# A fourth accumulator bank for the down projection, and both ends of the output projection reordered

## The chip, the cores and the metric

The kernel runs on one NeuronCore of a Trainium2 chip. The metric is the device time of one execution in microseconds (us). Matmuls run on TensorE (PE in the rows), elementwise work on VectorE (DVE), ScalarE (ACT) and GpSimd (POOL); SyncE (SP) and ACT issue the loads and stores. Matmul results land in PSUM, which this kernel uses as eight accumulators (banks) of 512 fp32 columns.

## What is computed

One decoder block over 2048 positions of width 1024, in fp32:

```
h = modulate(rms_norm(x, norm1_g[l]), shift1, scale1)
...
att_out = rms_norm(att, att_onorm_g[l])
mix = jnp.concatenate([hg_out, att_out], axis=-1) @ w_out[l]
x = x + gate1[:, None, :] * mix
h = modulate(rms_norm(x, norm2_g[l]), shift2, scale2)
a, u = jnp.split(h @ w_gate_up[l], 2, axis=-1)
x = x + gate2[:, None, :] * ((jax.nn.silu(a) * u) @ w_down[l])
return rms_norm(x, final_g)
```

`hg_out` is the output of a gated linear recurrence (512 columns), `att` that of a dilated attention (512 columns); `w_gate_up` has 2 x 2816 columns.

## The kernel before

Activations lie transposed: features on the partitions, positions along the free axis. Each fp32 matmul is made of three (lines 881 to 883 for most of the kernel, 1123 to 1125 for down): both operands are split into a high part (a cast on ACT) and a low part (a subtraction, `tt`, line 79, on DVE or POOL), and high x high, high x low and low x high are added in a bank. For a weight the parts are `whi` and `wlo`, made by `parts` from a loaded `wraw`.

The recurrence and the attention fill the first 1384 us. They leave their outputs in DRAM, `hg_d` and `at_d`, in four chunks of 512 positions. Then come:

**The output projection**, 1385 to about 1591 us: for each chunk c and each of eight row tiles j one bank (`psG`, four banks) takes 12 matmuls with the recurrence's half (`hgs`) and 12 with the attention's half (`ats`). The attention's half is first normed by `att_half`: a sum over partitions on TensorE (`norm_sum`, tile `nps`, in a bank of its own), `rstd` by Ln and Exp on ACT, the scaling on DVE (line 321), and the two parts of each of four tiles (cast `mx<-mraw` on ACT, line 291, and a subtraction on DVE). For chunk 0 four products are begun with the recurrence's half alone. Each finished bank is added to x on DVE (line 995), squared on ACT (line 305) and summed into `ssq`; at the start of the next chunk `norm_out` turns the chunk's rows into the FFN's input, which goes to DRAM as `h2_d`. In the last chunk the first operands of the FFN are loaded (`hr`, by `load_block`) and split by 28 *pieces* (`operand_pieces`), which run mostly on DVE; some of them first add or subtract operands, `hv<-hr` or `hr<-hr`.

**The FFN**, to the end: three pairs p of two position blocks (four blocks of 344 columns, then two of 336), and for each pair 11 steps g. A step has two `gate_up`, each of seven products of 12 matmuls (a 2 x 2 block scheme with sums and differences of weights, `wt`, and of operands), and one `down` for the step before: 16 groups of six matmuls, each in a bank (`psD`, three banks), which a residual step on DVE adds to x:

```
ps = pp_d.tile([P, CH], F32, name="psD", tag="psD", bufs=3)[:, 0:n]
...
dve.scalar_tensor_tensor(x, ps, ga2[:, j:j + 1], x, ALU.mult, ALU.add)
```

A `gate_up` ends with two `finish`: gate times up on DVE (`hm<-hm`), and the product's two parts (`ahi` on ACT, `alo<-hm,ahi` on DVE), which the next down needs. For the second `gate_up` of a step the parts are handed on as `late`, and `down` issues them at its fourth group (`soon`).

Each engine works through one queue in order. A scheduler sets that order when the program is built, from the order in which the source issues the steps, from priorities and from hints (`issue_after`, `keep_in_program_order`); the buffer counts of the pools (`bufs`) set when a tile is free again.

Of the kernel before, what the change touches and what calls it, by code (L numbers as in the profile page):

```python
# [19 lines left out]
P = 128  # L20
S = 2048
D = 1024
# [27 lines left out]
def hybrid_block(ctx, tc, xT, small, cst, w_ada, w_ft, w_tk, w_out, w_gu, w_dn, out):  # L50
# [233 lines left out]
    def load_mix(src):  # L284
        raw = cpool["mr"].tile([P, CH], F32, name="mraw", tag="mraw", bufs=6)
        nc.sync.dma_start(out=raw, in_=src)
        return raw

    def two_parts(dst, src, eng=dve, copy=act.copy):
        hi, lo = dst  # L290
        copy(hi, src)
        tt(eng, lo, src, hi.bitcast(F32), ALU.subtract)

    def norm_sum(ssq, n):
# [13 lines left out]
    def mix_tile(name):  # L308
        return cpool["mr"].tile([P, CH], F32, name="a" + name, tag="a" + name, bufs=2 if name == "sq" else 1)
# [7 lines left out]
    def att_half(dst, raws, ssq):  # L317
        rstd = mix_tile("sq")
        rstd_of(norm_sum(ssq, CH), rstd, 512)
        for k, raw in enumerate(raws):  # L320
            dve.scalar_tensor_tensor(raw, raw, sm[:, V_AG + k:V_AG + k + 1], rstd, ALU.mult, ALU.mult)
            two_parts(dst[k], raw)
# [358 lines left out]
    with ax:  # L681
# [30 lines left out]
        def branch_steps(hd):  # L712
# [36 lines left out]
            def drain():  # L749
                for br, bk, src in evac:  # L750
# [11 lines left out]
                    if hd == 7 and br == 0:  # L762
                        finish_head(hd, bk)
                        if bk == 0:
                            at(1, lambda: early.update(raws=[load_mix(at_d[k][0]) for k in range(4)]))
                            at(ATT, lambda: early.update(ssq=att_squares(early["raws"])))
# [66 lines left out]
        for hd in range(8):  # L833
# [13 lines left out]
            if hd == 7:  # L847
                hgs, raws, ws = {}, [], []
# [3 lines left out]
                def begin():  # L852
# [5 lines left out]
                    raws.extend(load_mix(hg_d[k][0]) for k in range(4))  # L858
                    raws.extend(raw_w(w_out[j][:, z * 512:(z + 1) * 512]) for j, z in FIRST)
                after[LAG + 2] = [begin]  # L860
                for k in range(4):
# [68 lines left out]


    h = {}
    with ExitStack() as wl:
        for nm in ("hg1", "at0", "xw0", "xw1", "at1", "wsc"):
            c_pool(nm, wl)
        for nm in ("pp_d", "ppc", "pp_n"):
            c_pool(nm, space=PSUM)

        def w_tile(name, bufs=2):
            return cpool["wsc"].tile([P, CH], F32, name=name, tag=name, bufs=bufs)  # L940

        def load_xw(c):
            x = cpool[f"xw{c % 2}"].tile([P, KT, CH], F32, name="xw", tag="xw")
# [4 lines left out]
        def norm_out(c, x, ssq):  # L948
            rstd = w_tile("rstd", 1)
            rstd_of(norm_sum(ssq, CH), rstd, D)  # L950
            for k in range(KT):
# [3 lines left out]
                nc.scalar.dma_start(out=h2_d[c][:, k, :], in_=v)  # L955

# [16 lines left out]
        for j in range(4):  # L973
            begun.append(psG(CH))
            product(begun[-1], wq[0, j][0], hgs[0], True, False)
        ats[0] = half_of("at0")
        att_half(ats[0], early["raws"], early["ssq"])
        pieces = []
        for i, (c, j) in enumerate(order):
# [11 lines left out]
            if c and j == 0:  # L991
                with tc.issue_after(end):
                    norm_out(c - 1, xs[c - 1], boxes[c - 1]["ssq"])
            x = xs[c][:, j, :]
            dve.scalar_tensor_tensor(x, ps, ga1[:, j:j + 1], x, ALU.mult, ALU.add)
            add_square(box, x, lambda name: w_tile(name, 1 if name == "ssq" else 2))
# [11 lines left out]
            if c + 1 < NCH:  # L1008
                if j == 3:
                    xs[c + 1] = load_xw(c + 1)  # L1010
                if j == 4:
                    ats[c + 1] = half_of(f"at{(c + 1) % 2}")
                    with tc.issue_after(end):
                        att_half(ats[c + 1], raws, ssq)
            if c == NCH - 1:
                if j == 0:
                    wr.close()
                    c_pool("hp", side="right")
                if j == 1:
                    n = BLK[0][1]  # L1020
                    tiles = [cpool[nm].tile([P, KT, CH], F32R if nm == "at0" else F32, name="hr", tag=tag)
                             for nm, tag in (("at0", "mx"), ("xw0", "xw"))]
                    tiles[0] = tiles[0].bitcast(F32)
# [245 lines left out]
```

## Time and profile before

| | |
|---|---|
| Median of 3 runs | 3075.54 us (3074.14 to 3080.18) |
| Profiled execution, its own time | 3070.15 us |
| Its span, first to last instruction | 3068.4 us |
| PE busy | 2850.8 us, 93% of the span, 16308 instructions |
| DVE busy | 2067.0 us, 67% |
| POOL busy | 1408.4 us, 46% |
| ACT busy | 1312.5 us, 43% |
| Mean granted TensorE clock | 0.979 of full speed |

Busy shares are means over the whole span. The chain that ended last is almost all PE's: its lines 881 to 883 come first, then 1123 to 1125. What a change in one stage is worth has to be read from that stage's waits.

### The profile page before, as it was taken

The page shows a single profiled execution, that of the slowest core. Times are in us where ns is not written, and L with a number is a line of the kernel's source. Part 1 is how long each engine was busy: PE and PEld are TensorE (multiplying, and loading weights), DVE is VectorE, ACT ScalarE, POOL GpSimd, SP SyncE. Part 2 cuts the span into 40 slices and gives each one's busy share as a digit, 9 for nine tenths or more (in the row PEclk, how much of TensorE's full clock was granted, in tenths as well). Part 3 has the DMA queues.
Part 4 walks back from the last instruction along what each step waited for, and adds up shares of the span by engine and source line. Part 5 has one row for each costly group of instructions (what it writes and reads, how often), then busy time and mean ns, then how long its engine had stood idle before and what let it go on. Part 6 is the DMA issues. An engine that isn't in the chain of part 4 may idle for free. (4 is left out here: it accounts for less than half of the span.)

```text
span 3068.4 us, 45120 instructions
## 1 busy us (share of the span) xinstructions
PE 2850.8 (93%) x16308; PEld 2595.3 (85%) x16308; DVE 2067.0 (67%) x3781; ACT 1312.5 (43%) x2388; POOL 1408.4 (46%) x1074
## 2 busy tenths in 40 slices
PE   6999998889899999998989999999999998999998
PEld 4777776667678999987769999998999998999997
DVE  7567566667644665666776666678667669776676
ACT  4533423334432565665554333345333335443334
POOL 5344422244533232320036566566566655665664
PEclk9999999999999999999989999999999999999999
DMA  6301336400238674537744222123232212231221
GB/s 243 118 35 42 117 124 219 151 32 32 83 115 218 143 165 101 134 106 237 260 161 157 73 80 79 60 83 106 96 116 73 80 66 95 83 113 63 81 71 67
DMA packets 212031, 343.32 MB, mean 112 GB/s; under 512 B 24784, under 2 KB 97360, under 8 KB 208720
## 3 DMA queue, kind: packets, MB, share of 16 engines
q1 hardware_dynamic: 201984, 322.35, 33.3%
q10 hardware_dynamic: 9824, 18.09, 1.6%
q8 instruction: 128, 2.10, 0.3%
q14 instruction: 95, 0.78, 0.1%
HBM read 281.39 MB, written 58.98 MB: 111 GB/s over the span
## 5 line engine op out<-in xcount | busy, mean ns | idle before, releaser
L79 POOL TENSOR_TENSOR wlo<-wraw,whi 128x512 fp32r<-128x512 f32 (+1 forms) x540 | 846.7, 1590 | 535.8 <-ACT whi L86 305.9
L881 PE MATMUL psG<-chi,whi 128*128 128x344 f32 (+1 forms) x1848 | 596.8, 323 | 15.6 <-DVE hm L79 7.4
L883 PE MATMUL psG<-chi,wlo 128*128 128x344 f32 (+1 forms) x1848 | 593.0, 321 | 3.5 <-POOL wlo L79 3.5
L882 PE MATMUL psG<-clo,whi 128*128 128x344 f32 (+1 forms) x1848 | 594.6, 322 | 0.0
L277 ACT CAST whi<-wraw 128x512 fp32r<-128x512 f32 x520 | 311.2, 619 | 423.7 <-issue 191.8
L1123 PE MATMUL psD<-ahi,whi 128*128 128x344 f32 (+1 forms) x1056 | 345.7, 327 | 43.8 <-DVE xc L1126 43.7
L1126 DVE SCALAR_TENSOR_TENSOR xc<-psD,mods,xc 128x344 f32<-128x344 f32 (+1 forms) x528 | 295.2, 569 | 110.0 <-PE psD L1125 109.8
L881 PEld LDWEIGHTS psG<-chi,whi 128*128 128x128 f32 x1848 | 351.2, 190 | 20.7 <-DVE hm L79 6.8
L883 PEld LDWEIGHTS psG<-chi,wlo 128*128 128x128 f32 x1848 | 350.5, 190 | 4.3 <-POOL wlo L79 4.1
L882 PEld LDWEIGHTS psG<-clo,whi 128*128 128x128 f32 x1848 | 350.2, 190 | 0.0
L79 POOL TENSOR_TENSOR wlo<-wt,whi 128x512 fp32r<-128x512 f32 x132 | 194.3, 1481 | 334.7 <-ACT whi L277 263.3
L1125 PE MATMUL psD<-ahi,wlo 128*128 128x344 f32 (+1 forms) x1056 | 337.3, 319 | 0.0
L1124 PE MATMUL psD<-alo,whi 128*128 128x344 f32 (+1 forms) x1056 | 336.3, 318 | 0.0
L79 DVE TENSOR_TENSOR hm<-hm,psG 128x344 f32<-128x344 f32 (+1 forms) x330 | 165.8, 503 | 244.3 <-PE psG L883 243.6
L511 PE MATMUL psA<-hhi,whi 128*128 128x512 f32 x640 | 262.7, 411 | 1.7 <-ACT hhi L396 1.7
L512 PE MATMUL psA<-hlo,whi 128*128 128x512 f32 x640 | 259.5, 406 | 0.2 <-DVE hlo L79 0.2
L513 PE MATMUL psA<-hhi,wlo 128*128 128x512 f32 x640 | 259.1, 405 | 0.0
L1123 PEld LDWEIGHTS psD<-ahi,whi 128*128 128x128 f32 x1056 | 198.8, 188 | 59.9 <-DVE xc L1126 55.5
L79 POOL TENSOR_TENSOR hd<-hb 128x256 f32<-128x256 f32 x192 | 134.2, 724 | 165.5 <-DVE hy L624 82.3
L1124 PEld LDWEIGHTS psD<-alo,whi 128*128 128x128 f32 x1056 | 199.0, 188 | 0.5
L1125 PEld LDWEIGHTS psD<-ahi,wlo 128*128 128x128 f32 x1056 | 198.9, 188 | 0.0
L277 ACT CAST whi<-wt 128x512 fp32r<-128x512 f32 x132 | 81.2, 617 | 258.9 <-DVE wt L79 139.0
(237 smaller groups left out, 6023.5 us busy)
## 6 DMA issues: line engine op xcount, KB each, us to landing
wraw<-in_w_gu SPq DMA_DIRECT2D x264, 256.0 KB
wraw<-in_w_dn SPq DMA_DIRECT2D x132, 256.0 KB
adaw<-in_w_ada SPq DMA_DIRECT2D x48, 512.0 KB
wraw<-in_w_ft SPq DMA_DIRECT2D x40, 512.0 KB
wraw<-in_w_tk SPq DMA_DIRECT2D x32, 512.0 KB
qk_d<-st SPq DMA_DIRECT2D x64, 256.0 KB
v<-v_d SPq DMA_DIRECT2D x16, 1024.0 KB
wraw<-in_w_out SPq DMA_DIRECT2D x64, 256.0 KB
```

What stands on the lines that cost most here:

```text
L79: return eng.tensor_tensor(o, a, b, op)
L277: copy(hi, raw)
L511: pe.matmul(ps, whi[:, ws], hhi[:, k, :], start=k == 0, stop=False)
L512: pe.matmul(ps, whi[:, ws], hlo[:, k, :], start=False, stop=False)
L513: pe.matmul(ps, wlo[:, ws], hhi[:, k, :], start=False, stop=k == 7)
L881: pe.matmul(ps, w[0][:, ws], hi, start=start and k == 0, stop=False, skip_group_check=True)
L882: pe.matmul(ps, w[0][:, ws], lo, start=False, stop=False, skip_group_check=True)
L883: last = pe.matmul(ps, w[1][:, ws], hi, start=False, stop=stop and k == 3, skip_group_check=True)
L1123: pe.matmul(ps, w[z][0][:, ws], ahi, start=z == 0, stop=False)
L1124: pe.matmul(ps, w[z][0][:, ws], alo, start=False, stop=False)
L1125: pe.matmul(ps, w[z][1][:, ws], ahi, start=False, stop=z == 1)
L1126: dve.scalar_tensor_tensor(x, ps, ga2[:, j:j + 1], x, ALU.mult, ALU.add)
```

## The change

1. `finish` no longer multiplies at once: the two products of gate and up become the first two entries of `late`, the parts the last two, and `down` takes one entry of `soon` at each group from the third on. (In the first `gate_up` of a step all four run at its end, as before.)
2. `psD` has four banks. The bank of `nps` is given up, and `norm_sum` takes one of the four in turn.
3. Start of the output projection: the first three attention tiles of chunk 0 are loaded and squared earlier; their norm is issued behind the second begun product, not the fourth, and the recurrence's tiles of the next chunk are split only after the attention's parts (`last_part`).
4. End: the `hr` tiles get room of their own and are loaded at j = 0 of the last chunk, four pieces follow each later j, the first product of the FFN (`gate_first`) is issued with the end of the stage, and the eight steps of `norm_out` for the last chunk come behind the first `gate_up`, with a load of ACT's function table.
5. Tiles share names (`rstd` lies in `ssq`, the FFN's small tiles in the projection's pool), and x tiles of odd chunks lie in a pool that the FFN goes on using.

```diff
-        raw = cpool["mr"].tile([P, CH], F32, name="mraw", tag="mraw", bufs=6)
+        raw = cpool["mr"].tile([P, CH], F32, name="mraw", tag="mraw", bufs=7)
...
     def norm_sum(ssq, n):
-        ps = cpool["pp_n"].tile([P, CH], F32, name="nps", tag="nps", bufs=1)[:, 0:n]
+        ps = cpool["pp_d"].tile([P, CH], F32, name="nps", tag="psD", bufs=4)[:, 0:n]
         pe.matmul(ps, ones, ssq, start=True, stop=True)
         return ps
+
+    def rstd_from(ps, dst, width, load):
+
+
+        if load:
+            with tc.issue_after(silu[0]):
+                tc.keep_in_program_order(act.preload_act_table_set("natural_log_exp_and_others"))
+        i = act.activation(dst, ps, AF.Ln, bias=eps, scale=1.0 / width)
+        if load:
+            tc.keep_in_program_order(i)
+        act.activation(dst, dst, AF.Exp, scale=-0.5)
...
                     raws.extend(load_mix(hg_d[k][0]) for k in range(4))
+                    early["raws"].extend(load_mix(at_d[k][0]) for k in range(3))
                     raws.extend(raw_w(w_out[j][:, z * 512:(z + 1) * 512]) for j, z in FIRST)
...
+    def gate_first(f, h, n):
+
+        raws = [raw_w(w_gu[i][:, z * 512:(z + 1) * 512]) for i, z in ((f, 0), (FT + f, 0), (FT + f, 1), (f, 1))]
+        ps = psG(n)
+        return raws, ps, product(ps, parts(raws[0]), h["11"])
...
-            product(begun[-1], wq[0, j][0], hgs[0], True, False)
-        ats[0] = half_of("at0")
-        att_half(ats[0], early["raws"], early["ssq"])
+            end = product(begun[-1], wq[0, j][0], hgs[0], True, False)
+            if j == 1:
+                ats[0] = half_of("at0")
+                with tc.issue_after(end):
+                    rstd = att_rstd(box["ssq"])
+        last_part = att_half(ats[0], early["raws"], rstd)
...
                 if j < 2:
-                    for k in (2 * j, 2 * j + 1):
-                        two_parts(hgs[c + 1][k], raws[k])
+
+                    with tc.issue_after(last_part):
+                        for k in (2 * j, 2 * j + 1):
+                            two_parts(hgs[c + 1][k], raws[k])
...
                 else:
-                    for _ in range(min(5, len(pieces))):
+                    for _ in range(4):
                         pieces.pop(0)()
-        norm_out(NCH - 1, xs[NCH - 1], box["ssq"])
-        while pieces:
-            pieces.pop(0)()
+        assert not pieces
+        first = gate_first(0, h, n)
...
-            def finish(si, u):
-
-                tt(dve, si, si, u, ALU.mult)
-                res.append(a_tile(n))
-                late.append(lambda: two_parts(dst, si))
-                dst = res[-1]
...
+            def finish(i, si, u):
+
+                def mul():
+                    tt(dve, si, si, u, ALU.mult)
+                    res.append(a_tile(n))
+                late.insert(i, mul)
+                late.append(lambda: two_parts(res[i], si))
+
...
-                if step == 4:
-                    for f in soon:
-                        f()
+                if step > 1 and soon:
+                    soon.pop(0)()
...
-                ps = pp_d.tile([P, CH], F32, name="psD", tag="psD", bufs=3)[:, 0:n]
+                ps = pp_d.tile([P, CH], F32, name="psD", tag="psD", bufs=4)[:, 0:n]
...
-                acts = [gate_up(2 * g, h, n)[0]]
+                acts = [gate_up(2 * g, h, n, first=None if p or g else first)[0]]
+                if not p and not g:
+                    steps = norm_out(NCH - 1, xs_last, boxes[NCH - 1]["ssq"], True)
```

The built order on three engines shows what the scheduler makes of it. On DVE, at one down call in the steady loop of the first pair (`hm<-hm` is gate times up, `hm<-hm,psG` takes a product's bank in, `xc<-psD,mods,xc` is the residual step), the rows before are:

```order
L79 TENSOR_TENSOR hm<-hm,psG 128x344
L79 TENSOR_TENSOR hm<-hm 128x344
L1126 SCALAR_TENSOR_TENSOR xc<-psD,mods,xc 128x344
L79 TENSOR_TENSOR alo<-hm,ahi 128x344
L1126 SCALAR_TENSOR_TENSOR xc<-psD,mods,xc 128x344
L79 TENSOR_TENSOR alo<-hm,ahi 128x344
L1126 SCALAR_TENSOR_TENSOR xc<-psD,mods,xc 128x344 x14
```

The rows of the changed kernel at the same place, on DVE:

```order
L79 TENSOR_TENSOR hm<-hm 128x344
L79 TENSOR_TENSOR hm<-hm,psG 128x344
L79 TENSOR_TENSOR hm<-hm 128x344
L1169 SCALAR_TENSOR_TENSOR xc<-psD,mods,xc 128x344
L79 TENSOR_TENSOR alo<-hm,ahi 128x344
L1169 SCALAR_TENSOR_TENSOR xc<-psD,mods,xc 128x344
L79 TENSOR_TENSOR alo<-hm,ahi 128x344
L1169 SCALAR_TENSOR_TENSOR xc<-psD,mods,xc 128x344 x14
```

Nothing moved here: the products stand ahead of the first residual step in both, and the parts between the first three.

On ACT, at the start of the output projection (`at_d` and `rl` belong to the attention's last head, `asq` is the attention's norm, `whi` a weight's part, `mx` a part of either half), before:

```order
L824 ACTIVATE rl<-rl 64x512
L827 DMA at_d_3_120<-ao 64x512
L277 CAST whi<-wraw 128x512
L291 CAST mx<-mraw 128x512 x2
L277 CAST whi<-wraw 128x512 x3
L91 ACTIVATE asq<-nps,eps 128x512
L92 ACTIVATE asq<-asq 128x512
L291 CAST mx<-mraw 128x512 x6
```

And of the changed kernel, on ACT at the same place:

```order
L840 ACTIVATE rl<-rl 64x512
L843 DMA at_d_3_120<-ao 64x512
L277 CAST whi<-wraw 128x512 x2
L91 ACTIVATE asq<-nps,eps 128x512
L92 ACTIVATE asq<-asq 128x512
L291 CAST mx<-mraw 128x512
L277 CAST whi<-wraw 128x512
L291 CAST mx<-mraw 128x512 x2
L277 CAST whi<-wraw 128x512
L291 CAST mx<-mraw 128x512 x5
```

The norm (lines 91 and 92) moved ahead of all casts, and the two casts of chunk 1's recurrence tiles that stood ahead of it went behind the attention's.

On SP, which issues the loads, at the end of the output projection (`w_out` and `w_gu` are the weights of the projection and of gate and up, `hr` the first operands of the FFN), before:

```order
L271 DMA wraw<-in_w_out 128x512 x9
L945 DMA xw<-in_xT 128x512 x8
L271 DMA wraw<-in_w_out 128x512 x7
L894 DMA hr<-h_d_125 128x8x344
L271 DMA wraw<-in_w_out 128x512 x4
L271 DMA wraw<-in_w_gu 128x512 x2
L894 DMA hr<-h_d_125 128x8x168
L894 DMA hr<-h_d_126 128x8x176
L271 DMA wraw<-in_w_gu 128x512 x9
```

And of the changed kernel, on SP at the same place:

```order
L271 DMA wraw<-in_w_out 128x512 x9
L984 DMA xc<-in_xT 128x512 x8
L271 DMA wraw<-in_w_out 128x512 x11
L271 DMA wraw<-in_w_gu 128x512 x5
L917 DMA hr<-h_d_125 128x8x344
L917 DMA hr<-h_d_125 128x8x168
L917 DMA hr<-h_d_126 128x8x176
L271 DMA wraw<-in_w_gu 128x512 x2
```

All three operand loads now stand together, behind five weight loads of gate_up; before, the first stood among the projection's weights and the other two behind two.

## Rows read from the trace of the kernel before

**Rows 1.** Windows: length, busy us (x instructions) by engine, PE clock, DMA share, GB/s.

```profile
1423.60:1576.60 153.00, 153.00 (x651) 122.06 (x649) 110.23 (x173) 91.78 (x155) 3.98 (x4) 1.00 0.70 239
1576.60:1621.00 44.40, 28.66 (x126) 25.36 (x126) 35.13 (x53) 24.58 (x44) 23.36 (x16) 0.77 0.28 95
1621.00:3068.40 1447.40, 1376.67 (x8613) 1354.88 (x8611) 1026.30 (x1513) 556.74 (x1079) 876.96 (x618) 0.99 0.26 86
```

**Rows 2.** Waits of PE from 1600 us on: total us, times, longest.

```profile
PE psD L1123 <- DVE xc L1126: 43.7, 39, 2.4
```

**Rows 3.** Timeline of PE, a down call: start, us, instruction [idle before <-releaser].

```profile
1918.75 0.32 PE L1123 MATMUL psD<-ahi,whi 128*128 128x344 f32 x1
...
1921.42 0.31 PE L1125 MATMUL psD<-ahi,wlo 128*128 128x344 f32 x1
1923.05 0.43 PE L1123 MATMUL psD<-ahi,whi 128*128 128x344 f32 x1 [1.32 <-DVE xc L1126]
...
1924.11 0.43 PE L1123 MATMUL psD<-ahi,whi 128*128 128x344 f32 x1
```

**Rows 4.** Timeline of DVE, the same call.

```profile
1919.93 1.60 DVE L79 TENSOR_TENSOR hm<-hm 128x344 f32<-128x344 f32 x1
...
1922.42 0.57 DVE L1126 SCALAR_TENSOR_TENSOR xc<-psD,mods,xc 128x344 f32<-128x344 f32 x1
...
1923.49 0.57 DVE L1126 SCALAR_TENSOR_TENSOR xc<-psD,mods,xc 128x344 f32<-128x344 f32 x1
```

**Rows 5.** Timeline of DVE, then of PE, a call of the second pair.

```profile
2191.69 0.51 DVE L79 TENSOR_TENSOR hm<-hm 128x344 f32<-128x344 f32 x1
...
2193.72 0.42 PE L1123 MATMUL psD<-ahi,whi 128*128 128x344 f32 x1 [0.20 <-DVE xc L1126]
2195.24 0.42 PE L1123 MATMUL psD<-ahi,whi 128*128 128x344 f32 x1 [0.32 <-DVE xc L1126]
```

**Rows 6.** Timeline of POOL, the call of rows 3.

```profile
1919.67 1.49 POOL L79 TENSOR_TENSOR wlo<-wt,whi 128x512 fp32r<-128x512 f32 x1 [0.38 <-ACT whi L277]
```

**Rows 7.** Timeline of PE, the start of the output projection.

```profile
1396.10 1.02 PE L296 MATMUL nps<-assq,ones 128*128 128x512 f32 x2
1404.77 2.07 PE L881 MATMUL psG<-mx,whi 128*128 128x512 f32 x4 [7.65 <-ACT mx L291]
...
1423.61 1.02 PE L296 MATMUL nps<-assq,ones 128*128 128x512 f32 x2
```

**Rows 8.** Timeline of ACT, then of DVE, the same stretch.

```profile
1397.15 0.69 ACT L91 ACTIVATE asq<-nps,eps 128x512 f32<-128x512 f32 x1 [0.47 <-PE nps L296]
...
1403.58 2.69 ACT L291 CAST mx<-mraw 128x512 fp32r<-128x512 f32 x5 [5.08 <-DMA mraw<-hg_d]
...
1398.53 2.08 DVE L321 SCALAR_TENSOR_TENSOR mraw<-mraw,sm,asq 128x512 f32<-128x512 f32 x3 [1.12 <-ACT asq L92]
```

**Rows 9.** Timeline of PE, the end of the output projection.

```profile
1583.31 0.80 PE L883 MATMUL psG<-mx,wlo 128*128 128x512 f32 x1 [6.50 <-DVE wlo L79]
...
1594.64 0.65 PE L881 MATMUL psG<-chi,whi 128*128 128x344 f32 x1 [2.15 <-ACT whi L277]
```

**Rows 10.** Timeline of PE, a down call of the last pair.

```profile
2768.34 0.42 PE L1123 MATMUL psD<-ahi,whi 128*128 128x336 f32 x1 [1.68 <-DVE xc L1126]
```

**Rows 11.** Timeline of DVE, the operand pieces' start and the weight sum behind them.

```profile
1569.56 0.94 DVE L79 TENSOR_TENSOR hv<-hr 128x344 f32<-128x344 f32 x2 [3.97 <-DMA hr<-h_d]
...
1591.66 0.68 DVE L79 TENSOR_TENSOR wt<-wraw 128x512 f32<-128x512 f32 x1
```

**Rows 12.** Timeline of SP's loads, the same stretch.

```profile
1561.00 6.17 SPq L271 DMA_DIRECT2D wraw<-in_w_gu  x4
```

**Rows 13.** Timeline of ACT, a table load.

```profile
1608.88 1.28 ACT L1088 ACT_TABLE_LOAD   x1 [0.39 <-ACT hv L954]
```

**Rows 14.** Timeline of DVE, then of PE, the end of the kernel.

```profile
3053.48 4.06 DVE L79 TENSOR_TENSOR ssq<-ssq,sq 128x336 f32<-128x336 f32 x4
...
3057.60 1.49 PE L296 MATMUL nps<-ssq,ones 128*128 128x336 f32 x2 [5.73 <-DVE ssq L79]
```

More of the change, by code (lines that the diff above doesn't have):

```diff
@@ L315, in att_squares, with att_rstd, att_half @@
         return box["ssq"]
-    def att_half(dst, raws, ssq):
+    def att_rstd(ssq):
         rstd = mix_tile("sq")
         rstd_of(norm_sum(ssq, CH), rstd, 512)
+        return rstd
+    def att_half(dst, raws, rstd):
         for k, raw in enumerate(raws):
             dve.scalar_tensor_tensor(raw, raw, sm[:, V_AG + k:V_AG + k + 1], rstd, ALU.mult, ALU.mult)
-            two_parts(dst[k], raw)
+            last = two_parts(dst[k], raw)
+        return last
     with ExitStack() as ab:
@@ L764, in drain @@
                         if bk == 0:
-                            at(1, lambda: early.update(raws=[load_mix(at_d[k][0]) for k in range(4)]))
-                            at(ATT, lambda: early.update(ssq=att_squares(early["raws"])))
+                            at(1, lambda: early["raws"].append(load_mix(at_d[3][0])))
+                            at(ATT, lambda: square(3))
                 evac.clear()
@@ L858, in begin @@
                     raws.extend(load_mix(hg_d[k][0]) for k in range(4))
+                    early["raws"].extend(load_mix(at_d[k][0]) for k in range(3))
                     raws.extend(raw_w(w_out[j][:, z * 512:(z + 1) * 512]) for j, z in FIRST)
                 after[LAG + 2] = [begin]
+                for k in range(3):
+                    after.setdefault(PRE - 1 + k, []).append(lambda k=k: square(k))
                 for k in range(4):
@@ L946, in load_xw, with norm_out, apply @@
             return x
[L948 to L951, printed above, removed]
+        def norm_out(c, x, ssq, load=False):
+            rstd = w_tile("ssq")
+            rstd_from(norm_sum(ssq, CH), rstd, D, load)
+            def apply(k):
                 v = w_tile("hv")
@@ L955, in norm_out @@
                 nc.scalar.dma_start(out=h2_d[c][:, k, :], in_=v)
+            return [lambda k=k: apply(k) for k in range(KT)]
         wq = {(0, j): [None, None] for j in range(4)}
@@ L1017, in hybrid_block @@
                     wr.close()
+                    w0.close()
+                    c_pool("hr", wl)
                     c_pool("hp", side="right")
-                if j == 1:
                     n = BLK[0][1]
-                    tiles = [cpool[nm].tile([P, KT, CH], F32R if nm == "at0" else F32, name="hr", tag=tag)
-                             for nm, tag in (("at0", "mx"), ("xw0", "xw"))]
-                    tiles[0] = tiles[0].bitcast(F32)
+                    tiles = [cpool["hr"].tile([P, KT, T], F32, name="hr", tag=f"hr{b}") for b in range(2)]
                     pieces = operand_pieces(h, [load_block(t, h2_d, b) for b, t in enumerate(tiles)], n,
@@ L1043, in a_tile, with gate_up @@
             return tuple(wk_a.tile([P, T], F32R, name=nm, tag=nm, bufs=8)[:, 0:n] for nm in ("ahi", "alo"))
-        def x_tiles(p):
-            return [cpool[f"xpc{p % 2}"].tile([P, KT, T], F32, name="xc", tag=f"xc{i}") for i in range(2)]
         def load_blocks(p, src_d):
-            return [load_block(t, src_d, 2 * p + i) for i, t in enumerate(x_tiles(p))]
+            pair = x_pair(p, 2 * T).rearrange("p (i k t) -> p i k t", i=2, t=T)
+            return [load_block(pair[:, i], src_d, 2 * p + i) for i in range(2)]
         pace = []
-        def gate_up(f, h, n, wait=False):
-            b11, b12 = raw_w(w_gu[f][:, 0:512]), raw_w(w_gu[FT + f][:, 0:512])
-            b22, b21 = raw_w(w_gu[FT + f][:, 512:1024]), raw_w(w_gu[f][:, 512:1024])
+        def gate_up(f, h, n, wait=False, first=None):
+            (b11, b12, b22, b21), p11, _ = first or gate_first(f, h, n)
             t1, t2 = [cpool["wk_h"].tile([P, 512], F32, name="wt", tag="wt", bufs=2) for _ in range(2)]
@@ L1132, in f_tile @@
         def f_tile(n):
-            return lambda name: cpool["wkc"].tile([P, T], F32, name=name, tag=name, bufs=2)[:, 0:n]
+            return lambda name: w_tile(name)[:, 0:n]
         def final_stats(box, x, j, n):
@@ L1140, in final_rstd @@
             ps = norm_sum(box["ssq"], n)
[L1141 to L1149 removed]
+            rstd = f_tile(n)("hv")
+            rstd_from(ps, rstd, D, load)
             box["rstd"] = rstd
```

58 lines of the change are left out of this document (32 added, 26 removed).

## The prediction

> **What bounds the kernel now.** I read the windows by stage first. From 1621 us to the end, the three pairs of the feed-forward network (FFN), TensorE is busy 1376.67 of 1447.40 us at a granted clock of 0.99, while DVE is busy 1026.30, ACT 556.74 and POOL 876.96 [rows 1]. TensorE sets the time there, and only its 70.7 idle us can be won. The same view shows three other stretches: the middle of the output projection runs without a gap (153.00 of 153.00 us, clock 1.00), and its end, 1576.6 to 1621.0, has TensorE busy for 28.66 of 44.40 us at clock 0.77: the two levels, 2.4 GHz (1.00) and 1.2 GHz (0.50), mixed, in a stretch where TensorE keeps waiting.
>
> Then the list of TensorE's waits: 43.7 us of the FFN's idle time, in 39 waits of at most 2.4 us, is the first matmul of a down group (L1123) waiting for the residual step on DVE (L1126) that empties its bank [rows 2].
>
> Then the timeline of one such call [rows 3]. The first down group starts at 1918.75, the last matmul of the third at 1921.42: 17 spacings of 0.157 us, so a group of six takes 0.943 us. The fourth group should start at 1921.58 and starts at 1923.05, 1.47 us late: the listed wait of 1.32 and 0.15 of restart. On DVE the first residual step runs only at 1922.42 (0.57 us), behind a product of gate and up (hm<-hm) that began at 1919.93 and took 1.60 [rows 4]. Such a product takes 0.51 elsewhere, at 2191.69; there the call has two waits of 0.20 and 0.32 instead of one of 1.32 [rows 5]. What differs is POOL: a weight split runs on it from 1919.67 for 1.49 us [rows 6], and both end within 0.4 us of each other. So the stall is one delayed product on DVE.
>
> Last the two ends of the output projection. At its start TensorE waits 7.65 us, to 1404.77, for a cast of attention parts on ACT [rows 7]; ACT had its Ln at 1397.15 and then stood 5.08 us for a load of chunk 1's hg, which the next four casts need, and the attention casts sit behind it [rows 8]. At its end TensorE waits 6.50 us for a weight part and 2.15 for another [rows 9].
>
> **The change, part by part.**
>
> *Products behind residual steps.* The source puts the two products behind two residual steps, but the built order on DVE reads the same row for row in the steady loop: both products still stand ahead of the first residual step. I cost this at nothing: the delayed product of [rows 4] stays where it is.
>
> *The fourth bank.* It lets the fourth group run while DVE is late. The fifth, due at 1918.75 + 4 x 0.943 = 1922.52, then waits for the bank that the first residual step frees at 1922.42 + 0.57 = 1922.99, so it starts about 1923.05. That is 0.53 late instead of 1.47: one group is bought, 0.943 us. The sixth, due at 1924.0, needs the step that ends at 1923.49 + 0.57 = 1924.06: no new stall. Of the 39 waits, 15 are of about 1.3 us like the one of [rows 3], four are of 1.96 to 2.40 (the longest in [rows 2]), and six are of about 1.7 in the last pair, whose 336 columns make a group 0.943 x 336 / 344 = 0.92 [rows 10]. Each of these 25 calls gains one whole group, 23.4 us together. Four calls have two short waits (0.20 + 0.32 and two restarts of 0.15, so 0.82 [rows 5]; in two of them about 0.3 more) and gain at most that, 3.4 together. The six small waits left stand in the changeovers between pairs, where the order also shifts a few rows; I give them nothing. Sum 26.8, called 27. Bounds: 46 if every wait and restart goes (43.7 less 2.2 of changeovers, and 0.15 for each of some 33 waits), and 0 if DVE falls behind by the group that it is given.
>
> *Start of the projection.* The sum for the attention norm moves on TensorE from behind the fourth half product to behind the second, so ahead by 24 matmuls; at the stage's 153.00 / 651 = 0.235 us [rows 1] that is 5.6 us, to about 1390.5. ACT gets Ln and Exp there and the attention casts before the four of chunk 1, so the load no longer blocks them. Before, the scaling on DVE began 2.43 us after the sum (1396.10 to 1398.53 [rows 7, 8]); a first cast follows in about 1.3 us, at 1394.2, the four chunks' parts take some 5 us on DVE (0.69 a step, two steps for each chunk), so the last is ready about 1399.5, where the matmuls, done with the half products at 1396.6, want it at 1398.7. I take 2.5 us lost, between 0 and 6 (6 if three loads put ahead of the weights on SP's queue make the half products late). What goes: 7.65, and the slow stretch behind it, 72 matmuls in 18.84 us (1404.77 to 1423.61 [rows 7]) against 72 x 0.235 = 16.9: 1.9. So 9.6 - 2.5 = 7.
>
> *End of the projection.* All its weight parts go ahead of the operand pieces, so the 6.50 us wait goes. But TensorE's next FFN product stays behind all 28 pieces on DVE: before, they began at 1569.56 when the second operand load landed, and the weight sum that follows them began at 1591.66 [rows 11]. The loads themselves now stand behind five gate_up weight loads on SP, not two; four of those took 6.17 us to issue [rows 12], so three cost about 4.6. Against that about 2.5 us of pieces need only the first load, and 0.7 of weight parts has left the stretch. So the product that started at 1594.64 [rows 9] comes some 1.5 us later. Behind it the last chunk's norm steps leave DVE and ACT until gate_up(0) is over; the waits of 2.94 and 1.62 there, and POOL's share of them, should shrink by 2 to 3. I take a gain of 1, between -6 (loads late, nothing recovered) and +10 (of the 15.7 idle us in the stretch [rows 1]). Two more table loads on ACT, 1.28 us each [rows 13], lie under TensorE, since ACT is idle over half of the FFN; uncovered they would cost 2.6.
>
> *Tail.* The norm sum now shares down's banks, so its place in the last down is fixed two groups earlier; TensorE may wait some 1.5 us there for the squares. DVE bounds the end (four sums from 3053.48 for 4.06 us, the last norm matmul at 3057.60 [rows 14]) and can use part of that pause: -1, between -3 and 0. The rest (one more raw buffer, tiles shared under other names, pools moved) adds no instruction to TensorE: 0.
>
> Sum: 27 + 7 + 1 - 1 = 34. The profiled execution took 3070.15 us, which is 5.4 under the median of the three runs; 3075.54 - 34 = 3041.5, said as 3041.
>
> **A rule weighed.** In [rows 4, 6] DVE's product, both of whose inputs lie in SBUF, takes 1.60 us while POOL splits weights, and 0.51 without that. The Trainium skill (SBUF — State Buffer, Who interferes with whom) says that a DVE instruction with two SBUF inputs and a GpSimd instruction that reads SBUF shut each other out, the first to start holding the shared port for its whole length, and that a DVE instruction with one SBUF input is not held. By that rule a residual step, which reads PSUM and one SBUF tile, put ahead of the product would not be late at all and the whole stall would go; the row agrees on the product, and the built order does not put the step ahead. That is rival 1.
>
> **The rivals.**
> 1. *The whole stall goes.* The products run late enough in fact, or the shift of TensorE by 0.94 us moves POOL's split off DVE's product, as at 2191.69 [rows 5]. FFN 46 in place of 27: 3022. For it: the four calls without the collision. Against: POOL and DVE follow TensorE's pace, so the collision moves along.
> 2. *The bank buys nothing.* DVE's later rows slip as well and the stall returns at the next group: 7 left, 3068.5, at the edge of what can be measured. Against: after the stall DVE waits for TensorE again within three groups, so it has slack.
> 3. *The end of the projection loses.* The loads behind the weights cost 6 instead of 1.5, the waits behind them don't shrink, and TensorE, pausing longer, runs more of its products at the 1.2 GHz level, as it does in that stretch now: 10 worse in all, 3052.
> 4. *Slower: the clock.* Without its pauses TensorE could be granted less in the FFN. 34 us are eaten once 1376.67 x (0.99 / c - 1) = 34, so it decides below c = 0.966; at 0.95 58 us are lost, and the time is 3099. Against: 153.00 us without a pause ran at 1.00 [rows 1].
>
> **How the numbers follow.** Forecast 0.60 (its own range 3033 to 3050), rival 1 0.13, rival 2 0.12, rival 3 0.11, rival 4 0.04. The range must leave out no more than 0.2: from rival 1's 3022 to 3058, which takes in rival 3 and leaves out 2 and 4. 0.2% of this kernel is 6 us, about what a measurement can tell from no change. Rival 2 lies at that border and is split between faster and same; 4 is slower: 0.89 faster, 0.07 same, 0.04 slower.
>
> **What would show it.** Right: in the FFN the waits of L1123 fall to about 0.4 us each and some 15 us in all, at the fifth group; a loop iteration shortens by about 0.94 us; DVE's product still takes 1.60; TensorE's wait near 1404 is under 3 us; the stretch from the projection's last half product to the second gate_up is as long as before within 6 us. Wrong: waits of 1.3 at the fifth group (rival 2), none at all (rival 1), a DVE that first idles for the operand loads more than 6 us longer (rival 3), a clock under 0.97 from 1621 on (rival 4).

## The result, and the profile after

The changed kernel takes 3039.61 us (median of 4 runs, 3036.97 to 3044.40), the kernel before 3074.84 (median of 4): a ratio of 0.9889, interval 0.9871 to 0.9906. The profiled execution of the changed kernel took 3040.49 us, its span is 3038.7.

The waits of TensorE from 1600 us on, in the profile after (us in total, times, longest):

```profile
PE psG L904 <- DVE hm L79: 18.4, 13, 3.9
PE psD L1166 <- DVE xc L1169: 15.8, 32, 1.4
PE nps L297 <- DVE ssq L79: 5.4, 2, 3.3
```

The stall of down's first matmul, 43.7 us in 39 waits in [rows 2], is 15.8 in 32, with TensorE busy for 1375.52 of the last 1426.70 us (window: length, busy us by engine, clock, DMA share, GB/s), where [rows 1] had 1376.67 of 1447.40:

```profile
1612.00:3038.70 1426.70, 1375.52 (x8594) 1352.56 (x8592) 1023.84 (x1521) 563.08 (x1087) 870.93 (x615) 0.99 0.27 86
```

But the wait for `hm`, the additions of gate_up's products on DVE, is 18.4 us in 13 waits, where the same view of the kernel before has 7.4 in 8:

```profile
PE psG L881 <- DVE hm L79: 7.4, 8, 2.4
```

The timeline of one down call after, PE, then DVE, then POOL (start us, us, instruction [idle before <-releaser]), answers to [rows 3, 4, 6]:

```profile
1913.75 0.32 PE L1166 MATMUL psD<-ahi,whi 128*128 128x344 f32 x1
1915.22 0.43 PE L1166 MATMUL psD<-ahi,whi 128*128 128x344 f32 x1 [0.36 <-DVE xc L1169]
...
1912.11 1.60 DVE L79 TENSOR_TENSOR hm<-hm 128x344 f32<-128x344 f32 x1
...
1914.60 0.57 DVE L1169 SCALAR_TENSOR_TENSOR xc<-psD,mods,xc 128x344 f32<-128x344 f32 x1
...
1911.84 1.49 POOL L79 TENSOR_TENSOR wlo<-wt,whi 128x512 fp32r<-128x512 f32 x1 [0.38 <-ACT whi L277]
```

The call begins at 1910.92, so the fourth group starts at 1913.75 without a wait, and the fifth waits 0.36 us. The product still takes 1.60 beside POOL's split, and the residual step still stands behind it.

The starts of a few instructions divide the time by stage. The last column is the stage after less the stage before:

| from - to | before | after | difference |
|---|---|---|---|
| start of the program - first half product | 1385.14 | 1386.88 | +1.74 |
| - second attention norm (start of the projection) | 38.47 | 30.67 | -7.80 |
| - norm of chunk 2 (middle) | 115.47 | 115.47 | 0.00 |
| - second FFN product (end of the projection) | 55.56 | 54.39 | -1.17 |
| - first down call | 61.69 | 68.80 | +7.11 |
| - last down call | 1364.72 | 1336.41 | -28.31 |
| - end | 47.31 | 46.07 | -1.24 |

At the start of the projection the wait for the cast is gone, as the timelines of PE and ACT show:

```profile
1391.58 0.50 PE L904 MATMUL psG<-mx,whi 128*128 128x512 f32 x1 [1.72 <-DVE acc L79]
1394.45 1.02 PE L297 MATMUL nps<-assq,ones 128*128 128x512 f32 x2
...
1417.55 1.02 PE L297 MATMUL nps<-assq,ones 128*128 128x512 f32 x2
...
1395.51 0.69 ACT L91 ACTIVATE asq<-nps,eps 128x512 f32<-128x512 f32 x1 [0.16 <-PE nps L297]
...
1405.11 0.62 ACT L291 CAST mx<-mraw 128x512 fp32r<-128x512 f32 x1 [1.44 <-DMA mraw<-hg_d]
```

ACT still stands for a chunk 1 load, 1.44 us where it was 5.08 [rows 8], but behind the attention's casts. One wait of 1.72 is new, for a bank that the attention's last sums (`acc`) free.

At the end of the projection the timelines of PE and DVE read:

```profile
1584.59 2.07 PE L297 MATMUL nps<-ssq,ones 128*128 128x512 f32 x2 [9.61 <-DVE ssq L79]
1587.41 0.65 PE L904 MATMUL psG<-chi,whi 128*128 128x344 f32 x1 [0.75 <-ACT whi L277]
...
1563.72 1.80 DVE L79 TENSOR_TENSOR clo<-hr,chi 128x344 fp32r<-128x344 f32 x4 [5.20 <-ACT chi L291]
...
1586.03 0.68 DVE L79 TENSOR_TENSOR wt<-wraw 128x512 f32<-128x512 f32 x1
```

TensorE's waits of 6.50 and 2.15 in [rows 9] have become one of 9.61 and one of 0.75: the pieces on DVE, 1563.72 to 1586.03, end the stage, 22.3 us in place of the 22.1 of [rows 11].

What was lost lies behind it, in the first steps of the FFN. Timelines of PE, DVE and SP:

```profile
1631.08 0.43 PE L904 MATMUL psG<-chi,whi 128*128 128x344 f32 x1 [1.92 <-DVE hm L79]
1652.63 0.63 PE L904 MATMUL psG<-chi,whi 128*128 128x344 f32 x1 [3.92 <-DVE hm L79]
...
1631.77 0.69 DVE L79 TENSOR_TENSOR hv<-xc,ssq 128x512 f32<-128x512 f32 x1 [0.75 <-DMA h_d<-hv]
...
1651.37 0.69 DVE L79 TENSOR_TENSOR wt<-wraw 128x512 f32<-128x512 f32 x1 [5.47 <-DMA wraw<-in_w_gu]
...
1641.94 0.52 SPq L917 DMA_DIRECT2D xc<-h_d  x1
1643.03 6.33 SPq L271 DMA_DIRECT2D wraw<-in_w_gu  x4
1649.41 0.52 SPq L917 DMA_DIRECT2D xc<-h_d  x1
```

The last chunk's norm steps (`hv<-xc,ssq`) stand on DVE among the additions for which TensorE waits; one of them itself waits for a store to free its tile. And DVE stands 5.47 us for a weight of the fifth gate_up: the loads of the second pair's operands (`xc<-h_d`) stand on SP among gate_up's weight loads, while before they stood behind these, among down's. These loads hang on the norm steps: since the change, chunk 3's x lies in the buffer that they fill (`x_pair`), and the first of them starts at 1641.94, once the last norm step on DVE has ended at 1640.35.

Of the 7.11 us lost there, 5.4 are idle time of TensorE (10.49 us in place of 5.08) and 1.7 are matmuls that take longer. Behind the wait of 3.92, from 1652.63 to 1656.21, twelve matmuls stand 0.29 us apart, where they stand 0.157 apart in [rows 3]. The granted clock of the window that takes in the end of that wait and these matmuls is 0.66, between the two levels of 1.00 (2.4 GHz) and 0.50 (1.2 GHz):

```profile
1649.00:1656.20 7.20, 3.57 (x12) 3.60 (x13) 4.46 (x7) 0.74 (x2) 4.19 (x4) 0.66 0.99 310
```

### The profile page after: what moved, and what is told of

Same layout as the page of the kernel before. It is cut to its first block, busy times and chain, and to the rows that moved or that the text cites. A ratio compares the mean times of both kernels' runs of the same rounds, so it can differ in the third digit from the quotient of the medians.

```text
span 3038.7 us, 45120 instructions
## 1 busy us (share of the span) xinstructions
PE 2847.3 (94%) x16308; PEld 2592.1 (85%) x16308; DVE 2063.4 (68%) x3781; ACT 1314.0 (43%) x2390; POOL 1411.9 (46%) x1074
## 5 line engine op out<-in xcount | busy, mean ns | idle before, releaser
L904 PE MATMUL psG<-chi,whi 128*128 128x344 f32 (+1 forms) x1848 | 597.5, 323 | 20.3 <-DVE hm L79 18.4
L1166 PE MATMUL psD<-ahi,whi 128*128 128x344 f32 (+1 forms) x1056 | 345.5, 327 | 16.3 <-DVE xc L1169 15.8
```

Of the source, the lines that this page charges most:

```text
L904: pe.matmul(ps, w[0][:, ws], hi, start=start and k == 0, stop=False, skip_group_check=True)
L1166: pe.matmul(ps, w[z][0][:, ws], ahi, start=z == 0, stop=False)
```

## The experiments

In the profiles of the changed kernel and its variants the first half product starts anywhere between 1376.81 and 1387.14 us, though nothing was edited ahead of it, and the middle of the projection is 115.47 us in every one. So the stages are compared from the profiles, and the table counts from the first half product; the medians stand beside it with their ratio to the kernel before on the same chip.

| kernel | start of proj. | end of proj. | to first down | first half product to end | median | ratio (interval) |
|---|---|---|---|---|---|---|
| before | 38.47 | 55.56 | 61.69 | 1683.22 | 3074.84 | |
| changed | 30.67 | 54.39 | 68.80 | 1651.81 | 3039.61 | 0.9889 (0.9871-0.9906) |
| three_banks | 30.40 | 54.24 | 70.84 | 1684.79 | 3069.69 | 0.9992 (0.9979-1.0005) |
| before_four_banks | 39.25 | 55.52 | 61.73 | 1658.12 | 3041.22 | 0.9902 (0.9882-0.9923) |
| products_behind | 30.66 | 53.93 | 70.61 | 1632.66 | 3015.16 | 0.9815 (0.9792-0.9837) |
| products_three_banks | 30.43 | 54.59 | 68.06 | 1633.75 | 3020.68 | 0.9824 (0.9806-0.9843) |
| start_back | 38.81 | 54.29 | 70.43 | 1661.39 | 3047.08 | 0.9918 (0.9900-0.9936) |
| loads_late | 30.71 | 53.99 | 64.05 | 1662.81 | 3049.46 | 0.9927 (0.9909-0.9944) |
| norm_ahead | 30.64 | 54.09 | 61.75 | 1647.96 | 3028.50 | 0.9855 (0.9836-0.9874) |
| spread_only | 30.69 | 54.36 | 63.90 | 1651.86 | 3034.04 | 0.9874 (0.9858-0.9891) |
| norm_held | 30.67 | 53.81 | 58.71 | 1632.68 | 3018.60 | 0.9819 (0.9805-0.9834) |
| products_spread | 30.64 | 54.51 | 58.35 | 1614.16 | 2997.34 | 0.9749 (0.9730-0.9767) |

**Is it the bank?** The changed kernel without it, and the kernel before with nothing else.

```diff
-        ps = cpool["pp_d"].tile([P, CH], F32, name="nps", tag="psD", bufs=4)[:, 0:n]
+        ps = cpool["pp_n"].tile([P, CH], F32, name="nps", tag="nps", bufs=1)[:, 0:n]
...
-                ps = pp_d.tile([P, CH], F32, name="psD", tag="psD", bufs=4)[:, 0:n]
+                ps = pp_d.tile([P, CH], F32, name="psD", tag="psD", bufs=3)[:, 0:n]
```

> The changed kernel with three banks for down and a bank of its own for the norm sum, as before; all else of the change stays. Theory (the bank buys one group per stalled call, the put-off products do nothing since the built order is the same): the waits of the first down matmul return to about 43 us in all, and the time is about 27 us above the changed kernel, 3067 us (3064 to 3070). Rival (the source's put-off of the products carries part of the gain): waits well under 43 us and a time under 3058.

```diff
-        ps = cpool["pp_n"].tile([P, CH], F32, name="nps", tag="nps", bufs=1)[:, 0:n]
+        ps = cpool["pp_d"].tile([P, CH], F32, name="nps", tag="psD", bufs=4)[:, 0:n]
...
-                ps = pp_d.tile([P, CH], F32, name="psD", tag="psD", bufs=3)[:, 0:n]
+                ps = pp_d.tile([P, CH], F32, name="psD", tag="psD", bufs=4)[:, 0:n]
```

> The kernel before with nothing changed but four banks for down, one of which the norm sum takes in turn. Theory (bank alone): about 27 us less than before, 3048 us (3045 to 3051), with waits of about 0.36 us at the fifth group of each down call. Rival (the gain needs the rest of the change): 3060 or more.

TensorE's waits from 1600 us on, first of three_banks, then of before_four_banks:

```profile
PE psD L1166 <- DVE xc L1169: 41.6, 39, 2.3
```

```profile
PE psD L1123 <- DVE xc L1126: 18.7, 33, 1.9
```

With three banks the stall is back at 41.6 us, 39 waits, and the time is that of the kernel before: the interval holds 1. With four banks alone the kernel before gains nearly what the whole change gains (0.9902 against 0.9889); the stages show 25.1 us of it (1683.22 to 1658.12), close to the 27 expected, while its median, 3041.22, fell below the expected 3045 to 3051. From the first half product on, the rest of the change without the bank is 1.6 us slower than before (1684.79 against 1683.22): what the start wins, the first steps of the FFN lose. No gain is left there that the put-off products could carry.

**What if the products do run behind residual steps?** The edit makes DVE do what the source asks for:

```diff
-                dve.scalar_tensor_tensor(x, ps, ga2[:, j:j + 1], x, ALU.mult, ALU.add)
+                added = dve.scalar_tensor_tensor(x, ps, ga2[:, j:j + 1], x, ALU.mult, ALU.add).ins
...
                 if step > 1 and soon:
-                    soon.pop(0)()
+                    with tc.issue_after(added):
+                        soon.pop(0)()
```

> The changed kernel with the two products of gate and up forced on DVE behind the second and the third residual step of down, which the source asks for and the built order does not do. Theory (the delayed product is the stall, a residual step is never held up itself): the waits of the first down matmul in the steady loop go from 15.8 us to under 4, and with the restarts the time falls by 14 to 19 us, to 3021 to 3026. Rival 1 (the product, held up behind two steps, delays the third step and the stall returns at the sixth or seventh group): 3035 to 3040. Rival 2 (the parts come late for the next call): waits for the parts' tiles, over 3040.

The same on the kernel with three banks:

> Three banks for down and a bank of its own for the norm sum, as before, but the products forced behind the second and third residual step. Theory (the late residual step is the whole stall, so three banks are enough once it is in time): waits of the first down matmul under 6 us in all and 42 us less than with three banks alone, within 4 us of the kernel with four banks and the same order, 3012 to 3020. Rival (both are needed: the third residual step, now behind a delayed product, stalls the sixth group): waits of 10 to 20 us, 3030 to 3040.

The waits of products_behind from 1600 us on:

```profile
PE psG L904 <- DVE hm L79: 19.8, 14, 3.9
PE nps L297 <- DVE ssq L79: 5.0, 2, 2.8
PE psD L1167 <- DVE xc L1170: 3.2, 8, 0.7
```

And the timelines of DVE and POOL in one down call of it:

```profile
1906.60 1.08 DVE L1170 SCALAR_TENSOR_TENSOR xc<-psD,mods,xc 128x344 f32<-128x344 f32 x2
1907.60 0.51 DVE L79 TENSOR_TENSOR hm<-hm 128x344 f32<-128x344 f32 x1
1908.05 0.58 DVE L1170 SCALAR_TENSOR_TENSOR xc<-psD,mods,xc 128x344 f32<-128x344 f32 x1
...
1905.93 1.50 POOL L79 TENSOR_TENSOR wlo<-wt,whi 128x512 fp32r<-128x512 f32 x1 [0.39 <-ACT whi L277]
```

The theory held, and the gain was just above its range of 14 to 19: the stall falls to 3.2 us and the stretch from the first half product on by 19.2 us (the median by 24.5). The two first residual steps run beside POOL's split in 1.08 us together, and the product behind them, which starts after the split's end, takes 0.51. The waits of products_three_banks in the same view:

```profile
PE psD L1167 <- DVE xc L1170: 7.8, 12, 1.3
```

The order alone does it: with three banks the waits of down come to 7.8 us in 12 places, none of them between 1660 and 2000 us, and the time from the first half product on is within 1.1 us of the four banks' (1633.75 against 1632.66). That is 51.0 us less than three_banks, where 42 were expected; the waits, and the median of 3020.68, lie a little above what was expected (under 6, and 3012 to 3020). What is left of the waits stands in the changeovers between pairs and the first call behind each. In the steady loop the fourth bank hides one group of a delay that need not be there.

**What does the start of the projection gain?**

```diff
-            if j == 1:
+            if j == 3:
                 ats[0] = half_of("at0")
...
-                    with tc.issue_after(last_part):
-                        for k in (2 * j, 2 * j + 1):
-                            two_parts(hgs[c + 1][k], raws[k])
+                    for k in (2 * j, 2 * j + 1):
+                        two_parts(hgs[c + 1][k], raws[k])
```

> The changed kernel with the start of the output projection as before in two points: the attention's norm behind the fourth begun product, and chunk 1's recurrence tiles split without waiting for the attention's parts. Theory (the order on ACT and TensorE is what the start gains): the stretch from the first half product to the second attention norm, 30.67 us in the changed kernel and 38.47 before, goes back to 37 to 40, with a wait for a cast near 7 us; the time rises by 7 to 9 us, to 3047 to 3049. Rival (the earlier loads of the attention tiles bring it): the stretch stays under 33.

Timelines of PE and ACT in it:

```profile
1396.71 2.08 PE L904 MATMUL psG<-mx,whi 128*128 128x512 f32 x4 [5.88 <-ACT mx L291]
...
1395.52 2.18 ACT L291 CAST mx<-mraw 128x512 fp32r<-128x512 f32 x4 [3.30 <-DMA mraw<-hg_d]
```

The stretch is 38.81 us and the wait behind ACT's blocked cast is back. So the gain of the stage is the order on TensorE and ACT, the two points taken together; the earlier loads alone bring nothing (38.47 before).

**What do the first steps of the FFN lose?** Four kernels, each the changed one with a single edit. First the operand loads, held until step 6 (`newest` is the last weight load issued):

```diff
                 if g == 6 and p < 2:
-                    raw = load_blocks(p + 1, h2_d)
+                    with tc.issue_after(newest[0]):
+                        raw = load_blocks(p + 1, h2_d)
```

> The changed kernel with the loads of the second pair's operands held on SP until the weight loads of step 6 are issued. Theory (in the first pair's first steps TensorE's wait of 3.92 us comes from weight loads that stand behind these operand loads): that wait goes, 3 to 5 us less, 3035 to 3037. Rival (the wait comes from the norm steps on DVE): no change, 3039 to 3040.

Timelines of PE and SP in it, at the down call after these loads:

```profile
1867.16 0.66 PE L1168 MATMUL psD<-ahi,whi 128*128 128x344 f32 x1 [4.45 <-DVE xc L1171]
...
1847.08 3.25 SPq L919 DMA_DIRECT2D xc<-h_d  x3
1850.44 25.79 SPq L271 DMA_DIRECT2D wraw<-in_w_gu  x8
```

The wait of 3.92 went, and the stretch to the first down call fell by 4.8 us, as the theory has it. But the expectation for the time was wrong: 4.4 us came back in the first down call itself, and the loads, three together ahead of eight weight loads, cost 4.45 us in one wait at the down call behind them and some 5 us again in the second pair. From the first half product to the end it is 11 us more than in the changed kernel.

Then the norm steps where they stood before:

```diff
+        for f in norm_out(NCH - 1, xs[NCH - 1], boxes[NCH - 1]["ssq"]):
+            f()
         first = gate_first(0, h, n)
...
-                if not p and not g:
-                    steps = norm_out(NCH - 1, xs_last, boxes[NCH - 1]["ssq"], True)
```

> The changed kernel with the last chunk's norm steps issued ahead of the first product of the FFN, as before, not behind the first gate_up. Theory (their DVE and ACT work in the first steps of the FFN, and the operand loads that they let go late, make the stretch from the second FFN product to the first down call 7 us longer than before, 68.8 against 61.7): it falls to 62 to 65, and the time by 4 to 6 us, to 3034 to 3036. Rival (only the position of the operand loads matters, which stay among the weight loads): 67 to 69, no change in the time.

The stretch is 61.75 us, as before the change (61.69), and the end of the projection does not grow (54.09). The operand loads start once the last norm step has ended, here at 1605.26 and 1611.88 among gate_up's weight loads, and TensorE has no wait for `hm` in the stretch: that they stand among weight loads is not enough for the loss. The first down call behind it gives back 3, so from the first half product on 3.9 us are won; the median fell by 11, most of it ahead of that point (1378.54 against 1386.88).

Then the loads in four parts each, issued one by one from down's groups (`slow_blocks` makes the list):

```diff
-                if g == 6 and p < 2:
-                    raw = load_blocks(p + 1, h2_d)
+                if g == (1, 6)[p] if p < 2 else False:
+                    raw, loads = slow_blocks(p + 1, h2_d)
+                    steps += loads
```

> The changed kernel with one edit: the loads of a pair's first operands cut into four parts each and issued behind down's weight loads (of steps 1 and 2 in the first pair, from step 6 on in the second). The products and the norm steps stand as in the changed kernel. Theory (of the 7.1 us that the stretch from the second FFN product to the first down call lost, the loads carry the 3.92 us wait for late weights, the norm steps on DVE the rest): the stretch falls from 68.8 to 63 to 65 us, nothing comes back later, the time falls by 4 to 6 us. Rival (the loads carry all): 61 to 62. Rival (the parts crowd the weights later): waits over 2 us in a later down call and no gain.

```profile
1651.50 0.59 PE L1185 MATMUL psD<-ahi,whi 128*128 128x344 f32 x1 [3.46 <-DVE xc L1188]
```

That row is the timeline of PE in it: the 4.9 us won before the first down call come back in that call, which with one wait of 3.46 is 4.4 us longer, and the sum from the first half product on is unchanged (1651.86 against 1651.81). The median is lower only by what lies ahead. So the loads are not the cause by themselves: with them gone a weight is still late (DVE stands 2.12 us for one at 1643.27), and the wait only moves.

Then the interleaved steps held on DVE behind a residual step (with `added` as above). At the end of each of the first two pairs these steps are the next pair's operand pieces, so the edit holds them too, which the expectation does not say:

```diff
                 if extra and step % every == every - 1:
-                    extra.pop(0)()
+                    with tc.issue_after(added):
+                        extra.pop(0)()
```

> The changed kernel with one edit: what down interleaves with its groups, the last chunk's norm steps in the first pair and the finishing steps in the others, is held on DVE behind a residual step of that down call. The built order also puts the operand loads of the second pair behind down's first weight loads then. Theory (the norm steps on DVE delay the products' additions in the first gate_ups): the stretch from the second FFN product to the first down call falls from 68.8 to 58 to 61 us, since neither the norm steps nor the loads are in it, and the time by 8 to 11 us, to 3029 to 3032. Rival (the steps delay the residual steps where they now stand): waits over 2 us in the first down call, and the gain is given back.

```profile
1650.93 0.42 PE L1166 MATMUL psD<-ahi,whi 128*128 128x344 f32 x1 [1.19 <-DVE xc L1169]
```

This row, again of PE's timeline, is the first wait that it shows from 1595 us on: the stretch is 58.71 us, 10.1 less, the pair behind it gives nothing back, and the hold takes another 9.4 in the second pair and the two changeovers around it (3.9 from the first pair's last down calls to the second pair's first, 1.4 in the second pair, 4.1 on the way into the third). The finishing steps and the operand pieces are held there together; which of them brings how much was not tried apart. The time from the first half product on falls by 19.1 us, twice what was expected. The norm steps on DVE, with the loads that wait for them, are what the first steps lost.

**All of it together:**

> Four banks and the products forced behind residual steps, and the two suspects of the FFN's first steps put away together: the loads of a pair's first operands cut into four parts each and issued behind down's weight loads of steps 1 and 2 of the first pair (from step 6 on in the second), and the last chunk's norm steps on DVE held behind residual steps of the first down call. Theory: the stretch from the second FFN product to the first down call goes from 70.6 to 61 to 63 us with no wait over 1 us in it, nothing comes back in later calls, and the time is 6 to 9 us under the kernel with the order alone, 3006 to 3010. Rival (the loads come late or crowd the weights later, as when they stood at step 6 together): waits over 2 us at a later down call, 3015 or more.

The waits of products_spread from 1600 us on, and its window from the first to the last down call (length, busy us by engine, clock, DMA share, GB/s):

```profile
PE psD L1186 <- DVE xc L1189: 9.2, 13, 1.8
PE nps L299 <- DVE ssq L79: 4.9, 2, 2.7
```

```profile
1642.90:2951.00 1308.10, 1296.34 (x8190) 1285.47 (x8189) 920.65 (x1431) 528.33 (x1013) 826.71 (x584) 1.00 0.28 90
```

2997.34 us, 2.5% under the kernel before and 42 us under the changed one (37.7 from the first half product on). That is below the range expected: of the 18.5 us under products_behind, 12.3 lie in the stretch to the first down call and 5.9 between the down calls, most of it in the changeovers, which had not been counted. Not all of the expectation held, since 6 us of the wait for banks came back (9.2 against 3.2), nearly all of it in the changeovers, where the edit holds the operand pieces as well. TensorE is busy for 1296.34 of 1308.10 us.

## Why the prediction was right, and where it was not

The time came out 1.4 us from the forecast, and that closeness is in part luck: the median fell by 35.2 us, while from the first half product on the change won 31.4 in the profiles, against 34 forecast; the rest is scatter of the time ahead of these stages. The 31.4 in turn hold partly by cancelling, a loss at the end of the projection against gains at the bank and in the tail.

- **The fourth bank, 27 forecast:** 28.3 between the first and the last down call. The step held in its detail: one group per call (without the bank, in three_banks, a step with its call takes 0.95 us longer in the steady loop of the first pair), the fifth group 0.53 late as worked out, 0.36 of it a listed wait, the product unchanged at 1.60. The two kernels with and without the bank show that it is the bank: over the same stretch it is worth 25.6 us on the kernel before and 30.1 with the rest of the change.
- **The products put off, 0 forecast:** right, since the built order did not move them; three_banks shows no gain left for them.
- **The start of the projection, 7 forecast:** 7.8. The 2.5 us of lost time allowed for the attention's parts did not appear; the new wait of 1.72 for a bank took part of its place.
- **The end of the projection, +1 forecast:** this step failed. Its first half, the second FFN product 1.5 us later, came out 1.2 earlier. The second operand load was issued as late after the norm of chunk 2 as before (20.5 us against 20.4), so the five weight loads did not hold it up; its operand was first used 4.0 us later (34.5 against 30.5), near the 4.6 allowed, but the pieces of the first operand filled more of that time than allowed, and fewer pieces ran long beside POOL (from there on three of over 0.6 us on DVE, before five). Nor had all 28 pieces begun at 1569.56, as the prediction reads it: four on DVE had run from 1541.69 on. Its second half, "the last chunk's norm steps leave DVE and ACT until gate_up(0) is over; the waits ... should shrink by 2 to 3", had the wrong sign. The steps did not leave, they moved by one gate_up, into DVE's rows among the additions that TensorE waits for, and weights came late there: 7.1 us lost, so the step comes to -5.9 in all, at the edge of its bounds. norm_held shows the cause by taking it away: where the steps do leave, the stretch is 3.0 us shorter than in the kernel before (58.71 against 61.69), the size that the step had forecast, though the idle time gives only 0.7 of it and matmuls that take less time the rest. By which way the steps make the weights late (through DVE, or through POOL, which splits them) was not tried.
- **The tail, -1 forecast:** +1.2. The pause for the squares came, 2.16 us, but DVE used more than all of it to catch up: the last norm waits 3.25 in place of 5.73 [rows 14].

Timeline of PE at the end of the changed kernel:

```profile
3017.07 0.83 PE L297 MATMUL nps<-ssq,ones 128*128 128x336 f32 x2 [2.16 <-DVE ssq L79]
3028.55 0.83 PE L297 MATMUL nps<-ssq,ones 128*128 128x336 f32 x2 [3.25 <-DVE ssq L79]
```

Rival 1 did not happen in the changed kernel, but its first mechanism, products that run late enough, is the true one: once the order is forced, the stall of the steady loop goes. Rival 2 is out: the fifth group waits some 0.36 us in the first two pairs and 0.75 in the last, where the fourth had waited 1.3 and 1.7, and its two longest, 1.38 and 1.15 around the start of the third pair, were 2.32 and 2.33 before. Rival 3 came half true: the end lost 5.9 where 1 was to be gained, by waits and slower matmuls behind the stage as it says, but not by loads that hold up the stage itself. Rival 4 is out: the clock is 1.00 between the down calls even with no more than 11.8 us of pauses left in 1308 (products_spread).

The rule weighed in the prediction (the Trainium skill, SBUF — State Buffer, Who interferes with whom) agrees with the trace. In the changed kernel from 1700 us on, counted over its 344-column rows: 54 products `hm<-hm` start while POOL works and take 0.54 to 1.61 us, and every one of them ends 0.37 to 0.38 us after the POOL instruction that was running; 23 start while it does not and take at most 0.52; residual steps take 0.58 us at most in either case (64 and 272 of them).

## What to carry to other kernels

When an accumulator waits, look first at what stands ahead of the instruction that frees it, and for how long that is held up by another engine; reordering two rows on DVE was worth more than a bank (51.0 us against 33.0, both counted from three_banks). Read the built order before crediting an edit: here the source asked for an order that the scheduler did not make, and one explicit hold was worth 19 us. Work that is put off lands somewhere: before pricing it at a gain, read which rows it will stand among and who waits for those.

## What the runs showed that was not expected

The time ahead of the edited stages scatters by more than several of the effects: the first half product starts between 1376.81 and 1387.14 us in ten profiles of the changed kernel and its variants, and a median of four to twelve runs carries that along. spread_only's median is 5.6 us under the changed kernel's with no gain in the sum from the first half product on, while the 115.47 us in the middle of the projection repeat to 0.01 in all twelve kernels. At this size stage lengths from the trace decide, and medians only confirm.
